# A hybrid decoder step on one core: last products deferred past the next first product, the input copied from the transposes' banks, a row ring of 13, prompt stores begun by ScalarE

## The chip, the core and the metric

The kernel runs on one core of a Trainium2 chip. TensorE (PE in the tables, its weight loads PEld), VectorE (DVE), ScalarE (ACT), GpSimd (POOL) and SyncE (SP, which here only begins DMAs) each run their own list of instructions in order and wait for one another by semaphores. Matrix products are collected in PSUM, eight banks of 128 x 512 floats; everything else lies in SBUF. The metric is the time of one execution on the device in microseconds (us).

## The reference, cut to what matters

```python
def hybrid_layer(x, pos0, n_lead, pool_buf, C, n, m, ...):
    hn = rmsnorm(x, norm_g)
    proj = jnp.einsum('btd,dn->btn', hn, w_in)
    a_pool, z_pool, q, k, v, o, z_m, i_pre, f_pre, g_pool, g_mlstm = split_projection(proj)
    y_pool = multiscale_pool(pool_buf, a_pool, pos0, w_pool, pool_scale) * jax.nn.silu(z_pool)
    ...
    (C_new, n_new, m_new), h = mlstm_scan(qh, kh, vh, ig, lf, state, n_lead)
    ...
    y_mlstm = jax.nn.sigmoid(o) * h.astype(x.dtype) * jax.nn.silu(z_m)
    u = (jax.nn.sigmoid(g_pool) * jnp.einsum('btp,pd->btd', y_pool, w_branch_pool)
         + jax.nn.sigmoid(g_mlstm) * jnp.einsum('btm,md->btd', y_mlstm, w_branch_mlstm))
    x_out = x + jnp.einsum('btd,de->bte', u, w_out)
```

There are 560 tokens (16 meta, 512 of a prompt, 8 samples of 4), a model width of 1024, 4 heads of 512, and an input projection of 1024 x 14344 in float32. The outputs are the tokens, and the new states: the prompt's memories C (one 512 x 512 for each head) and those of the 8 samples, which are read, updated and written back.

## The kernel before

**Arithmetic.** Each float32 operand is split into a high part (a ScalarE cast) and a low part (a VectorE subtraction), and each product is three products of parts (`mm3`, whose matmuls all bear L166). `hT` holds the normalised input, transposed, as such a pair.

**Units.** The input projection is cut into units of 256 output columns. 47 are a `quad`: seven block products in place of eight, each of 12 matmuls with 272 columns, on sums of quarters of the input (`S`, parts a to d, made once by `quarter_sums`) and sums of weight blocks. In the order of the code they are p1, p2, p6, p5, p7, p3, p4. Three banks carry them. The last one, p4 (weights `wb`, input `hT`), adds to bank A only after VectorE has read that bank for the total "22" (L253) and before ScalarE writes it out as "21" (L284). A total writes a tile that later goes to DRAM; where the tile's slot last held something that is being stored, VectorE waits for that store, and p4 for VectorE. The units of the v projection (L974, L977) are ordinary products.

**Stages.** `begin` normalises and transposes five tiles of tokens. The transposes stand in PSUM; `parts` in it casts `hT_hi` on ScalarE and subtracts `hT_lo` on VectorE from those banks (L80). `projections_begin` runs the first a unit, the gates (L573 and the single rows on four partitions, L577 to L641), the quarter sums and the v units of head 0, and the casts of z unit 0. `quarter_sums` first lets GpSimd add `hT_hi` and `hT_lo` to four tiles x (L539), then VectorE combine them (L542). `projections` walks over the other units; each is woven with the operands of the next, with the stores of the one before, and with the sample memories (`sample_C`, L1121 and L1130 on TensorE, L1135 on VectorE). `attention` runs the four heads, the pooling branch and the mLSTM branch follow, and the output product ends the kernel.

**Order.** TensorE's order inside the stages is that of the code (a manual schedule); `weave` interleaves lists of steps evenly. Instructions made through `Pinned` (`pA`, `pV`) keep the code's order too. The other engines are ordered by a scheduler, but each then runs its list strictly in order: an instruction that waits holds all behind it, and a DMA that SyncE cannot begin yet holds all later DMAs of SyncE.

**Rings.** Tiles are taken from rings of slots: "r" (12 slots of 128 x 560: q, k, v and c as they come or go, and y), "row" (9 slots of 128 x 544 in a head: `D2` with the denominators, `og` with the gated outputs, `sqn` with the squares). A new tile waits until the old one in its slot is done with. In a head, GpSimd sums the decay rows to `D2` (L1411 to L1416), these are split to dh and dl (L140), and TensorE sums them over partitions (L1399). The new prompt memory of a head is made in four row blocks: TensorE (L1358), a copy c32 by ScalarE (L1361), and a store begun by SyncE (L1362).

Of the kernel before, what the change touches and what calls it, by code (L numbers as in the profile page):

```python
# [23 lines left out]
H = 4  # L24
# [59 lines left out]
class Unit:  # L84
# [3 lines left out]
    def __init__(self, load=(), ahead=(), products=(), after=(), then=()):  # L88
        self.load, self.ahead, self.products = list(load), list(ahead), list(products)
        self.after, self.then = list(after), list(then)  # L90

# [8 lines left out]
class Trunk:  # L100
# [85 lines left out]
    def quad(self, src, lo, dst, scale=None, f21=None, after=(), then=()):  # L186
# [98 lines left out]
        return Unit([load], ahead, [p1, p2, p6, p5, p7, p3, p4], after, then)  # L285
# [77 lines left out]
    def begin(self):  # L363
# [29 lines left out]
        self.hT = [ip.tile([P, NK, NT], F32R, name=n) for n in ("hT_hi", "hT_lo")]  # L393
        self.hS = ip.tile([P, NK, 112], F32R, name="hS")
# [50 lines left out]
        def parts(*js):  # L445
            pieces = []
            for j in js:
                for q in range(2):
                    pv = pss[j, q].rearrange("p (k t) -> p k t", k=4)
                    for s, n, c0 in COLS[j]:  # L450
                        pieces.append((pv[:, :, s:s + n], *(t[:, 4 * q:4 * q + 4, c0:c0 + n] for t in self.hT)))
# [79 lines left out]
    def quarter_sums(self):  # L531
        nc = self.nc
        V, A, G = nc.vector, nc.scalar, nc.gpsimd
        steps, x = [], {}

        def load(k0, half, kh):
            t = x[half, kh] = self.gp.tile([P, 2, HN], F32, tag=f"x{half}{kh}", name=self.name("x"), bufs=1)
            hi, lo = (t[:, 4 * kh + k0:4 * kh + k0 + 2, HN * half:HN * half + HN].bitcast(F32) for t in self.hT)
# [12 lines left out]
        for k0 in (0, 2):  # L551
            steps += [lambda k0=k0, t=t: load(k0, *t) for t in (a, c, b, d)]
            steps += [lambda: sums(ALU.subtract, a, c, a), lambda: sums(ALU.subtract, c, b, c),
                      lambda: sums(ALU.subtract, b, a, b), lambda: sums(ALU.add, d, d, b)]
            for s, t in ("a", a), ("b", b), ("c", c), ("d", d):
                steps += [lambda k0=k0, s=s, t=t, l=l: part(k0, s, t, l) for l in (False, True)]
        return steps


    def gates(self):  # L560
# [22 lines left out]
        V.scalar_tensor_tensor(az, z, -1.0, z, ALU.mult, ALU.max)  # L583
# [39 lines left out]
        for i in (3, 2, 1, 0):  # L623
            own = TILE0[i] + P - TSTART[i]
            V.tensor_copy(sv[i][:, :own], nQ[:, TSTART[i]:TSTART[i] + own])

            V.tensor_scalar(sv[i][:, own:], sv[i + 1][:, :SEGW[i] - own],
                            b[:, TILE0[i] + P - 1:TILE0[i] + P], None, ALU.add)
            yield
        for i in range(5):  # L630
            c0 = TILE0[i]
            c1 = c0 + (P if i < 4 else 16)
            last = (SEGW[i] if i < 4 else 16) - 1
            V.tensor_scalar(wsr[:, c0:c1], a[:, c0:c1], sv[i][:, last:last + 1], None, ALU.add)
            yield
# [24 lines left out]
    def projections_begin(self):  # L660
# [7 lines left out]
        for f in v[0].ahead + a.products:  # L668
            f()
        for n, u in enumerate(v):  # L670
# [16 lines left out]
    def projections(self, rest):  # L687
# [46 lines left out]
        loaded, C, outs = 0, {}, []  # L734
# [5 lines left out]
        for t, u in enumerate(units):  # L740
# [20 lines left out]
        for f in before.after + old.then + before.then + outs:  # L761
            f()
# [186 lines left out]
    def unit_v(self, h):  # L949
# [8 lines left out]
        def part(kk, low):  # L958
# [3 lines left out]
            else:  # L962
                (G if h == 0 and kk % 2 else V).tensor_tensor(w[kk][2], w[kk][0], w[kk][1].bitcast(F32), ALU.subtract)
# [237 lines left out]
    def attention(self):  # L1201
# [15 lines left out]
        for h, u in enumerate(heads):  # L1217
# [21 lines left out]
    def head(self, h):  # L1239
# [15 lines left out]
        def row(name):  # L1255
            return self.hp.tile([P, NO], F32, tag="row", name=self.name(name), bufs=9)
# [96 lines left out]
        def prompt_C(d):  # L1353
# [8 lines left out]
            nc.sync.dma_start(O["C_prompt"][0, 0, h, d * P:(d + 1) * P], c32)  # L1362
# [134 lines left out]
    def y_in(self, yy, k, src):  # L1497
        nc = self.nc
        t = self.r("y32")[:, :NO]
        nc.sync.dma_start(t, src)  # L1500
# [12 lines left out]
    def pool_branch(self):  # L1513
# [12 lines left out]
        for k in range(8):  # L1526
            self.y_in(self.yp2, k, self.yp_d[:, k])
# [8 lines left out]
    def final(self, up):  # L1536
# [4 lines left out]
        for m in range(16):  # L1541
            y_in(ym[m // 8], m % 8, self.y_d[:, m])
# [96 lines left out]
```

## Time and profile before

| | |
|---|---|
| median of 3 runs | 1148.51 us (1145.27 to 1151.25) |
| the profiled execution | 1146.45 us, of which 1144.6 us are the span of its instructions |
| TensorE busy | 1066.5 us (93%) |
| VectorE busy | 843.0 us (74%) |
| ScalarE busy | 533.5 us (47%) |
| GpSimd busy | 195.2 us (17%) |
| DMA | 233.33 MB, mean 204 GB/s |

One execution was recorded. A line of the timeline gives an instruction's start and duration and, in brackets, how long its engine had stood idle before it and whose work released it. The view of waits adds these up; the view of windows gives each engine's busy time in a stretch and the clock granted to TensorE (1.00 is full speed, 0.50 half). The chain follows the work that ended last back to the start.

### The profile page before, as it was taken

How to read it: one execution, taken by the hardware profiler on the slowest of the kernel's cores; microseconds unless marked ns; L12 is line 12 of the kernel's file. 1: busy time of each engine (PE TensorE's matmuls, PEld its weight loads, DVE VectorE, ACT ScalarE, POOL GpSimd, SP SyncE). 2: the span in 40 equal slices, each digit the busy share in tenths (PEclk: the TensorE clock that was granted, in tenths of full speed). 3: DMA queues.
4: the chain of work that ended last, by engine and by line, in shares of the span. 5: the costliest groups of instructions: out<-in, count | busy, mean ns of one | idle time of the engine just before them, and what ended most of it. 6: DMA issues, size and time to landing. Idle time of an engine off the chain costs nothing.

```text
span 1144.6 us, 19677 instructions
## 1 busy us (share of the span) xinstructions
PE 1066.5 (93%) x7390; PEld 961.5 (84%) x7390; DVE 843.0 (74%) x1346; ACT 533.5 (47%) x1003; POOL 195.2 (17%) x323
## 2 busy tenths in 40 slices
PE   7948999998999999999998999986999789999997
PEld 5848999967999968999868989975978679999976
DVE  5696888796789697889696888863699888534353
ACT  4455555333554435554444554455677555222232
POOL 3720120001210000400001300022454534100000
PEclk9978999998999999999999999997999899999999
DMA  8424456779656778657588567887677699522232
GB/s 214 149 51 122 136 166 203 256 235 275 214 182 219 238 257 236 212 178 249 186 266 262 167 223 268 282 280 259 205 264 248 203 310 353 174 74 75 66 116 83
DMA packets 159663, 233.33 MB, mean 204 GB/s; under 512 B 17369, under 2 KB 82133, under 8 KB 159561
## 3 DMA queue, kind: packets, MB, share of 16 engines
q1 hardware_dynamic: 159569, 232.09, 63.2%
q8 instruction: 58, 0.95, 0.3%
q14 instruction: 36, 0.29, 0.1%
HBM read 160.65 MB, written 70.93 MB: 202 GB/s over the span
## 4 chain that ended last, share of the span: by engine, by line
PE 68%; DMA 11%; DVE 9%; issue 4%; ACT 3%; POOL 3%; SPq 1%; DVEq 0%; POOLq 0%; ACTq 0%
PE ps L166 55%; PE ps L974 4%; DMA v_d<-v 3%; PE ps L1121 2%; DMA wraw<-in_w_in_dram 2%; PE ps L1358 2%; PE ps L1130 1%; DMA kw<-k_d 1%; DMA out_dram<-C 1%; POOL x L539 1%; ACT qc L1156 1%; DMA k<-k_d 1%; PE ps L1401 1%; PE ps L977 1%; DMA ra<-in_w_in_dram 1%
## 5 line engine op out<-in xcount | busy, mean ns | idle before, releaser
L166 PE MATMUL ps<-hT_hi,w 128*128 128x272 f32 (+1 forms) x752 | 159.0, 297 | 0.0
L166 PEld LDWEIGHTS ps<-hT_hi,w 128*128 128x128 f32 x752 | 125.3, 193 | 4.2 <-issue 2.4
L166 PE MATMUL ps<-hT_lo,w 128*128 128x272 f32 (+1 forms) x376 | 110.2, 293 | 0.0
L1135 DVE SCALAR_TENSOR_TENSOR C<-C,sw,ps 128x512 f32<-128x512 f32 x128 | 89.4, 741 | 12.1 <-PE ps L1130 11.8
L166 PE MATMUL ps<-Sb_hi,wb 128*128 128x272 f32 (+1 forms) x376 | 80.9, 295 | 17.5 <-DVE wb L205 15.6
L166 PE MATMUL ps<-hT_hi,wb 128*128 128x272 f32 (+1 forms) x376 | 82.7, 299 | 11.4 <-DVE q L253 7.7
L1044 POOL COPY qm<-qw 128x16 f32<-128x16 f32 x32 | 7.1, 254 | 430.4 <-DVE qw L1041 430.4
L166 PE MATMUL ps<-Sa_hi,wa 128*128 128x272 f32 (+1 forms) x376 | 79.9, 292 | 0.0
L166 PE MATMUL ps<-Sc_hi,wa 128*128 128x272 f32 (+1 forms) x376 | 78.9, 290 | 0.0
L166 PEld LDWEIGHTS ps<-Sb_hi,wb 128*128 128x128 f32 x376 | 63.2, 192 | 18.7 <-issue 16.0
L166 PE MATMUL ps<-Sd_hi,w 128*128 128x272 f32 (+1 forms) x376 | 78.7, 289 | 0.0
L202 ACT CAST wa<-ra 128x1024 fp32r<-128x1024 f32 x47 | 49.4, 1050 | 62.0 <-DVE ra L215 55.4
L205 DVE TENSOR_TENSOR wb<-rb,wb 128x1024 fp32r<-128x1024 f32 x47 | 57.7, 1227 | 24.6 <-ACT wb L202 24.3
L166 PEld LDWEIGHTS ps<-hT_hi,wb 128*128 128x128 f32 x376 | 64.5, 195 | 13.1 <-DVE q L253 8.4
L166 PEld LDWEIGHTS ps<-hT_lo,w 128*128 128x128 f32 x376 | 72.6, 193 | 0.0
L202 ACT CAST w<-rb 128x1024 fp32r<-128x1024 f32 x47 | 49.3, 1050 | 29.3 <-PE ps L166 16.2
L166 PEld LDWEIGHTS ps<-Sa_hi,wa 128*128 128x128 f32 x376 | 63.0, 191 | 0.0
L166 PEld LDWEIGHTS ps<-Sc_hi,wa 128*128 128x128 f32 x376 | 62.2, 189 | 0.0
L166 PEld LDWEIGHTS ps<-Sd_hi,w 128*128 128x128 f32 x376 | 61.9, 188 | 0.0
L205 DVE TENSOR_TENSOR w<-rb,w 128x1024 fp32r<-128x1024 f32 x47 | 57.3, 1220 | 4.3 <-ACT w L202 4.3
L205 DVE TENSOR_TENSOR wa<-ra,wa 128x1024 fp32r<-128x1024 f32 x47 | 57.5, 1224 | 0.0
L166 PE MATMUL ps<-hT_lo,wb 128*128 128x272 f32 (+1 forms) x188 | 55.8, 297 | 0.0
(372 smaller groups left out, 3115.6 us busy)
## 6 DMA issues: line engine op xcount, KB each, us to landing
C<-in_state_C_dram SPq DMA_DIRECT2D x64, 512.0 KB
out_dram<-C SPq DMA_DIRECT2D x64, 512.0 KB
ra<-in_w_in_dram SPq DMA_DIRECT2D x47, 512.0 KB
rb<-in_w_in_dram SPq DMA_DIRECT2D x47, 512.0 KB
wraw<-in_w_in_dram SPq DMA_DIRECT2D x18, 512.0 KB
v<-v_d SPq DMA_DIRECT2D x32, 256.5 KB
wraw<-in_w_branch_mlstm_dram SPq DMA_DIRECT2D x16, 512.0 KB
k_d<-k SPq DMA_DIRECT2D x16, 280.0 KB
```

The lines of the kernel that those rows point to most:

```text
L166: self.nc.tensor.matmul(out, s, m, start=(first and j == 0), stop=(j == len(seq) - 1), skip_group_check=not check)
L202: A.copy(w[name][0], w[s])
L205: V.tensor_tensor(w[name][1], w[s], w[name][0].bitcast(F32), ALU.subtract)
L539: G.tensor_tensor(t, hi, lo, ALU.add)
L974: nc.tensor.matmul(pv[i], s, m[:, k2], start=(k == 0 and j == 0), stop=(k == 7 and j == 2))
L977: nc.tensor.matmul(pv[4][:112], self.hS[:, k], m[:, k2], start=(k == 0 and j == 0), stop=(k == 7 and j == 1))
L1121: nc.tensor.matmul(self.pqc[h][r:r + 8], self.qm[h % 2][:, d, b], Cs[bb // 2][:, bb % 2], start=(d == 0 and g == 0), stop=(d == 3 and g == 1),
L1130: nc.tensor.matmul(pu, self.kwst[h, d][r:r + 12, g], self.vst[h][r:r + 12, g], start=True, stop=True, tile_position=(r, 0))
L1135: V.scalar_tensor_tensor(C, C, self.bview(self.sw[h][:, 0])[:, 4 * g + bb, 3:4], pu, ALU.mult, ALU.add)
L1156: A.activation(t[r, :HD], pqc[r], AF.Copy, accum_out=t[r, HD:])
L1358: nc.tensor.matmul(pc, w[:, s, i], vr[i][:, m], start=(i == 0 and j == 0), stop=False)
L1401: nc.tensor.matmul(pb[:, o:o + mv.shape[-1] - m], s, mv[:, m:], start=(j == 0), stop=(j == last[True]))
```

## The change

Four things change.

- A `quad` gets the mark `tail`. `projections` emits the first product p1 of a unit, then the p4 kept back from the unit before, then the rest; sample products (`extra`) now stand ahead of the rest. The first unit there, z unit 0, has a transposition appended to its products, so that this is what is kept back, and its p4 stays in place.
- `begin` makes a tile `X` (128 x 8 x 560) with the whole input, by 12 ScalarE copies from the transposes' banks (8 of 128 x 512, 4 of 128 x 96), after the casts and the subtractions. `quarter_sums` drops its 8 GpSimd additions and works in place on `X`; the 4 low parts of b and d (L547) and 2 of the low parts of v weights (L963) go from GpSimd to VectorE. Four steps of the gates stand ahead of the v units.
- In the gates, |z| (L583), the four copies L625 and the five additions L634 go from VectorE to ScalarE.
- The row ring grows from 9 to 13. The 16 prompt stores L1362 are begun by ScalarE. In the last head, two loads of the pooling branch's input are begun ahead of the numerators, and the last of its `rows` steps is woven with them.

```diff
-        return Unit([load], ahead, [p1, p2, p6, p5, p7, p3, p4], after, then)
+        u = Unit([load], ahead, [p1, p2, p6, p5, p7, p3, p4], after, then)
+        u.tail = True
+        return u
...
+        self.X = gp.tile([P, NK, NT], F32, name="X")
...
-            for src, hi, lo in pieces:
+            for src, hi, lo, x in pieces:
                 pA.copy(hi, src)
-            for src, hi, lo in pieces:
+            for src, hi, lo, x in pieces:
                 pV.tensor_tensor(lo, src, hi.bitcast(F32), ALU.subtract)
+            for src, hi, lo, x in pieces:
+                pA.copy(x, src)
...
-            G.tensor_tensor(t, hi, lo, ALU.add)
+            x[half, kh] = self.X[:, 4 * kh + k0:4 * kh + k0 + 2, HN * half:HN * half + HN]
...
-                (G if s in "bd" else V).tensor_tensor(lo, x[t], hi.bitcast(F32), ALU.subtract)
+                V.tensor_tensor(lo, x[t], hi.bitcast(F32), ALU.subtract)
...
-        V.scalar_tensor_tensor(az, z, -1.0, z, ALU.mult, ALU.max)
+        nc.scalar.activation(az, z, AF.Abs)
...
-            V.tensor_copy(sv[i][:, :own], nQ[:, TSTART[i]:TSTART[i] + own])
+            nc.scalar.copy(sv[i][:, :own], nQ[:, TSTART[i]:TSTART[i] + own])
...
-            V.tensor_scalar(wsr[:, c0:c1], a[:, c0:c1], sv[i][:, last:last + 1], None, ALU.add)
+            nc.scalar.activation(wsr[:, c0:c1], a[:, c0:c1], AF.Identity, bias=sv[i][:, last:last + 1])
...
-        for f in v[0].ahead + a.products:
+        for f in v[0].ahead + a.products + other[:4]:
             f()
+        other = other[4:]
...
             products = u.products
+            for f in products[:1] + tail:
+                f()
+            products, tail = products[1:], []
+            if u.tail:
+                products, tail = products[:-1], products[-1:]
             if t not in values:
-                products, extra = products[:1] + extra + products[1:], []
+                products, extra = extra + products, []
...
-                (G if h == 0 and kk % 2 else V).tensor_tensor(w[kk][2], w[kk][0], w[kk][1].bitcast(F32), ALU.subtract)
+                V.tensor_tensor(w[kk][2], w[kk][0], w[kk][1].bitcast(F32), ALU.subtract)
...
-                weave(u.rows[-2:], u.sums, last)
-            weave(u.numerators[:-1] if h == H - 1 else u.numerators, m.keys + m.values)
+                weave(u.rows[-2:-1], u.sums, last)
+            if h == H - 1:
+                self.yraw = [self.y_load(self.yp_d[:, k]) for k in range(2)]
+                weave(u.numerators[:-1] + u.rows[-1:])
+            else:
+                weave(u.numerators, m.keys + m.values)
...
-            return self.hp.tile([P, NO], F32, tag="row", name=self.name(name), bufs=9)
+            return self.hp.tile([P, NO], F32, tag="row", name=self.name(name), bufs=13)
...
-            nc.sync.dma_start(O["C_prompt"][0, 0, h, d * P:(d + 1) * P], c32)
+            nc.scalar.dma_start(O["C_prompt"][0, 0, h, d * P:(d + 1) * P], c32)
```

In `begin`, ScalarE's row of casts before was this (`hT_hi` from the transposes; `wg` is the gates' weight, loaded by a DMA):

```order
L80 CAST hT_hi<-ps_262 128x4x128
L80 CAST hT_hi<-ps_267 128x4x128
L80 CAST hT_hi<-ps_297 128x4x24 x2
L80 CAST hT_hi<-ps_302 128x4x24 x2
L137 CAST wg<-wg_raw 128x8x64
L961 CAST whi_408<-wraw_120 128x1024
```

and is now, on the same engine at the same place:

```order
L80 CAST hT_hi<-ps_272 128x4x128
L80 COPY X<-ps_249 128x4x128
L138 CAST wg<-wg_raw 128x8x64
L80 COPY X<-ps_254 128x4x128
L80 COPY X<-ps_267 128x4x128
L80 COPY X<-ps_272 128x4x128
L80 CAST hT_hi<-ps_302 128x4x24 x2
L80 CAST hT_hi<-ps_307 128x4x24 x2
L80 COPY X<-ps_302 128x4x24 x2
L80 COPY X<-ps_307 128x4x24 x2
L553 CAST Sa_hi<-X 128x560 x2
```

The casts of the last token tile moved behind the cast of `wg` and three copies.

On TensorE, at the end of the first q unit of head 1 (p3 on `Sd`, p4 on `wb`, then p1 of the next unit; ps are banks), the rows before were:

```order
L166 MATMUL ps_2952<-Sd_lo,w_424_2777 128x272
L166 MATMUL ps_2952<-Sd_hi,w_424_2777 128x272
L166 MATMUL ps_2892<-hT_hi,wb_2838 128x272
L166 MATMUL ps_2892<-hT_lo,wb_2837 128x272
...
L166 MATMUL ps_2892<-hT_hi,wb_2837 128x272
L166 MATMUL ps_3035<-hT_hi,w_443_2858 128x272
L166 MATMUL ps_3035<-hT_lo,w_443_2858 128x272
```

and are now:

```order
L167 MATMUL ps_2952<-Sd_hi,w_417_2780 128x272
L167 MATMUL ps_3017<-hT_hi,w_435_2858 128x272
L167 MATMUL ps_3017<-hT_lo,w_435_2858 128x272
...
L167 MATMUL ps_3017<-hT_hi,w_435_2858 128x272
L167 MATMUL ps_2888<-hT_hi,wb_2835 128x272
L167 MATMUL ps_2888<-hT_lo,wb_2834 128x272
```

The 12 matmuls of p1 moved between p3 and p4.

On GpSimd, in the middle of `attention` (P are the decay matrices, D the row of denominators of head 2, klo low parts of keys), the rows before were:

```order
L140 TENSOR_TENSOR Pl_10326<-bc_9590,Ph_10325 128x144
L140 TENSOR_TENSOR Pl_10326<-bc_9590,Ph_10325 80x48
L140 TENSOR_TENSOR klo_10322<-k_1745_10319,khi_10321 128x560
L1411 TENSOR_TENSOR D_1764_10381<-bc_9590 128x400
L1412 COPY D_1764_10381<-bc_9590 128x112
L1413 COPY D_1764_10381<-qns 128x32
L140 TENSOR_TENSOR klo_10378<-k_1761_10375,khi_10377 128x560
L1416 TENSOR_TENSOR D_1764_10381<-D_1764_10381,bc_9590 128x272
```

and are now:

```order
L1425 TENSOR_TENSOR D_1756_10378<-bc_9587 128x400
L141 TENSOR_TENSOR Pl_10312<-bc_9587,Ph_10311 128x400
L1430 TENSOR_TENSOR D_1756_10378<-D_1756_10378,bc_9587 128x272
...
L1430 TENSOR_TENSOR D_1756_10378<-D_1756_10378,bc_9587 48x48
L141 TENSOR_TENSOR klo_10319<-k_1737_10316,khi_10318 128x560
L141 TENSOR_TENSOR klo_10375<-k_1753_10372,khi_10374 128x560
```

The whole sum of D moved ahead of the two keys, among the decay matrices.

## Rows read from the trace of the kernel before

**Rows 1.** The page: busy time, share of the span and instructions of TensorE.

```profile
PE 1066.5 (93%) x7390; PEld 961.5 (84%) x7390; DVE 843.0 (74%) x1346; ACT 533.5 (47%) x1003; POOL 195.2 (17%) x323
```

**Rows 2.** Waits of TensorE: line, releaser's line; total us, times, longest.

```profile
PE ps L166 <- DVE q L253: 7.7, 3, 3.5
...
PE ps L166 <- ACT p L238: 1.8, 3, 0.6
```

**Rows 3.** Windows: stretch, length, busy us by engine, clock, DMA share, GB/s.

```profile
97.00:272.00 175.00, 172.98 (x1230) 154.11 (x1230) 142.45 (x226) 84.08 (x146) 11.51 (x37) 0.98 0.62 196
778.00:800.00 22.00, 13.12 (x48) 9.75 (x47) 10.58 (x20) 11.58 (x28) 3.73 (x4) 0.69 0.88 287
...
945.00:1144.00 199.00, 191.45 (x1355) 180.16 (x1354) 98.49 (x148) 56.46 (x90) 23.11 (x29) 1.00 0.41 134
```

**Rows 4.** Timeline of TensorE: start, us, instruction, idle before and releaser.

```profile
82.70 0.57 PE L166 MATMUL ps<-Sb_hi,wb 128*128 128x272 f32 x1 [15.61 <-DVE wb L205]
94.67 0.39 PE L166 MATMUL ps<-hT_hi,wb 128*128 128x272 f32 x1 [3.00 <-DVE zx L253]
...
277.14 0.60 PE L166 MATMUL ps<-hT_hi,wb 128*128 128x272 f32 x1 [2.65 <-DVE q L253]
...
789.32 0.77 PE L166 MATMUL ps<-qh,klo 128*128 128x512 f32 x1 [5.44 <-ACT qh L137]
...
903.35 0.54 PE L1399 MATMUL ps<-dl,ones 128*128 128x240 f32 x1 [8.49 <-DVE dl L140]
935.33 0.82 PE L166 MATMUL ps<-yp,wlo 128*128 128x272 f32 x2 [4.71 <-ACT yp L137]
```

**Rows 5.** The chain that ended last: start, us, what (matmuls counted).

```profile
94.67 2.36 PE ps L166 x12
...
113.78 34.98 PE ps L166 x276
...
277.14 11.82 PE ps L166 x70
...
783.11 6.06 DMA out_dram<-c
```

**Rows 6.** Timeline of ScalarE, start of the kernel.

```profile
23.83 0.90 ACT L80 CAST hT_hi<-ps 128x96 fp32r<-128x96 f32 x4 [1.35 <-PE ps L80]
30.63 0.62 ACT L137 CAST wg<-wg_raw 128x512 fp32r<-128x512 f32 x1 [5.90 <-DMA wg_raw<-in_w_in_dram]
```

**Rows 7.** Timeline of VectorE, first 97 us.

```profile
32.31 1.40 DVE L963 TENSOR_TENSOR wlo<-wraw,whi 128x1024 fp32r<-128x1024 f32 x1 [5.50 <-ACT whi L961]
39.63 5.25 DVE L542 TENSOR_TENSOR x<-x,x 128x560 f32<-128x560 f32 x4 [5.92 <-POOL x L539]
44.79 0.73 DVE L547 TENSOR_TENSOR Sa_lo<-x,Sa_hi 128x560 fp32r<-128x560 f32 x1
...
57.76 1.93 DVE L583 SCALAR_TENSOR_TENSOR az<-zf 4x560 f32<-4x560 f32 x1
...
80.96 0.46 DVE L634 TENSOR_SCALAR ws<-ga,rw 4x128 f32<-4x128 f32 x2
81.35 1.21 DVE L205 TENSOR_TENSOR wb<-rb,wb 128x1024 fp32r<-128x1024 f32 x1
```

**Rows 8.** Timeline of SyncE: DMAs begun in the attention.

```profile
780.76 0.34 SPq L1362 DMA_DIRECT2D out_dram<-c  x1
...
931.13 0.35 SPq L1231 DMA_DIRECT2D out_dram<-np_out  x1
931.52 3.83 SPq L1500 DMA_DIRECT2D y<-yp_d  x8
```

**Rows 9.** Timeline of GpSimd in the attention.

```profile
893.68 1.45 POOL L1411 TENSOR_TENSOR D<-bc 128x400 f32<-128x400 f32 x1 [3.17 <-DVE og L1470]
...
896.48 1.84 POOL L140 TENSOR_TENSOR klo<-k,khi 128x560 fp32r<-128x560 f32 x1
```

**Rows 10.** The page: groups; line engine op, busy, mean ns, idle before.

```profile
L1135 DVE SCALAR_TENSOR_TENSOR C<-C,sw,ps 128x512 f32<-128x512 f32 x128 | 89.4, 741 | 12.1 <-PE ps L1130 11.8
```

More of the change, by code (lines that the diff above doesn't have):

```diff
@@ L90, in __init__ @@
         self.after, self.then = list(after), list(then)
+        self.tail = False
 def weave(*lists):
@@ L450, in parts @@
                     for s, n, c0 in COLS[j]:
-                        pieces.append((pv[:, :, s:s + n], *(t[:, 4 * q:4 * q + 4, c0:c0 + n] for t in self.hT)))
-            for src, hi, lo in pieces:
+                        pieces.append((pv[:, :, s:s + n], *(t[:, 4 * q:4 * q + 4, c0:c0 + n] for t in (*self.hT, self.X))))
+            for src, hi, lo, x in pieces:
                 pA.copy(hi, src)
-            for src, hi, lo in pieces:
+            for src, hi, lo, x in pieces:
                 pV.tensor_tensor(lo, src, hi.bitcast(F32), ALU.subtract)
+            for src, hi, lo, x in pieces:
+                pA.copy(x, src)
         def first(j):
@@ L534, in quarter_sums, with quarter @@
         steps, x = [], {}
-        def load(k0, half, kh):
-            t = x[half, kh] = self.gp.tile([P, 2, HN], F32, tag=f"x{half}{kh}", name=self.name("x"), bufs=1)
-            hi, lo = (t[:, 4 * kh + k0:4 * kh + k0 + 2, HN * half:HN * half + HN].bitcast(F32) for t in self.hT)
-            G.tensor_tensor(t, hi, lo, ALU.add)
+        def quarter(k0, half, kh):
+            x[half, kh] = self.X[:, 4 * kh + k0:4 * kh + k0 + 2, HN * half:HN * half + HN]
         def sums(op, out, p, q):
@@ L551, in quarter_sums @@
         for k0 in (0, 2):
-            steps += [lambda k0=k0, t=t: load(k0, *t) for t in (a, c, b, d)]
-            steps += [lambda: sums(ALU.subtract, a, c, a), lambda: sums(ALU.subtract, c, b, c),
+            steps += [lambda k0=k0: [quarter(k0, *t) for t in (a, c, b, d)], lambda: sums(ALU.subtract, a, c, a), lambda: sums(ALU.subtract, c, b, c),
                       lambda: sums(ALU.subtract, b, a, b), lambda: sums(ALU.add, d, d, b)]
@@ L733, in projections @@
         self.early = self.head(0)
-        loaded, C, outs = 0, {}, []
+        loaded, C, outs, tail = 0, {}, [], []
         before = Unit(after=rest[0].after + rest[1].after)
@@ L755, in projections @@
             products = u.products
+            for f in products[:1] + tail:
[3 more added lines that the diff above has]
+                products, tail = products[:-1], products[-1:]
             if t not in values:
-                products, extra = products[:1] + extra + products[1:], []
+                products, extra = extra + products, []
             weave(products, ahead, old.then + before.after, extra, done, self.gate_steps[t] if t < 2 else [])
             old, before = before, u
-        for f in before.after + old.then + before.then + outs:
+        for f in tail + before.after + old.then + before.then + outs:
             f()
@@ L1495, in both, with y_load, y_in @@
         return [pool.tile([P, 8, NO], F32R, tag="yy", name=f"{name}{j}", bufs=bufs) for j in range(2)]
-    def y_in(self, yy, k, src):
+    def y_load(self, src):
+        t = self.r("y32")[:, :NO]
+        self.nc.sync.dma_start(t, src)
+        return t
+    def y_in(self, yy, k, t):
         nc = self.nc
-        t = self.r("y32")[:, :NO]
-        nc.sync.dma_start(t, src)
         self.split(yy[0][:, k], yy[1][:, k], t, nc.scalar, nc.gpsimd if k % 2 else nc.vector)
```

4 lines of the change are left out of this document (2 added, 2 removed).

## The prediction, as it was recorded before the run

> **What bounds the kernel now.** I read the page first: TensorE is busy for 1066.5 of 1144.6 us [rows 1], so no edit that frees another engine pays unless it shortens one of TensorE's waits, or a stretch in which those waits have pulled its clock down. The 78 us without work are the whole stock. The waits of TensorE by releaser [rows 2] and its own timeline [rows 4] say where they lie; the windows [rows 3] say where they don't: from 97 to 272 us it is busy for 172.98 of 175, and from 945 us to the end at clock 1.00, so nothing that the change does elsewhere is worth anything there. The chain [rows 5] gives the price of a slow clock: 276 matmuls of the projections take 34.98 us, 0.127 each, while the 70 that follow the wait at 277.14 take 11.82, which is 11.82 - 70 x 0.127 = 2.9 too many. Four places are left: the end of the start (to 97 us), the three q waits, the first head of the attention, and the stretch from 893 to 945 us.
>
> **The start.** TensorE waits 15.61 us for the low part of `wb` and another 3.00 for zx before the last 12 matmuls, which end at 94.67 + 2.36 = 97.0 [rows 4, 5]. From the first of these waits' end that is 14.3 us for 60 matmuls; 60 x 0.127 are 7.6, the wait is 3.0, and the remaining 3.7 are slow clock.
>
> Against the change: ScalarE's cast of `wg` waits for a DMA and ends at 30.63 + 0.62 = 31.25 [rows 6]. The casts of the last token tile, which ended at 23.83 + 0.90 = 24.73, now stand behind it and three copies. A copy of 128 x 512 is not shown; the cast of this size took 0.62, so the casts end at about 31.25 + 3 x 0.62 + 0.9 = 34.0, 9.3 us later, and TensorE's products on those tokens wait for them. What hides this is the 15.61 us: 6.3 are left of them, some 3 if TensorE then runs at half clock for a while. The copies' sum, 8 x 0.62 + 0.9 = 5.9 us of ScalarE, lies in the same idle stretch.
>
> For it: VectorE's sums began at 39.63, after 5.92 us of waiting for GpSimd's additions [rows 7]. With the input in `X` they begin when the last copies are done, 34.0 + 0.9, so 4.7 us earlier. VectorE loses |z|, 1.93, and nine short gate rows at 0.46 / 2 = 0.23, 2.1 in all. It gains four low parts at 0.73 and two weight parts at 1.40, 5.7 in all. The eight sums took 5.25 for four beside GpSimd; the low part, of the same shape, took 0.73, so between nothing and 2 x (5.25 - 4 x 0.73) = 4.7 come back. The balance for `wb` is 4.7 + 1.9 + 2.1 - 5.7 = 3.0, up to 7.7 us earlier than 81.35. As TensorE's v products end later, and ScalarE must empty their banks between its casts, I take 2. Behind that, the 14.3 us shrink to 7.6 with neither wait nor slow clock, to 11.3 with the same clock; the tile that zx waits for is stored earlier by the same gate rows, and the idle time before is some 5 us and no longer 15.6, so I take 9.3. Gain 2 + 5 = **7**, from 0 (the later products eat both) to 7.7 + 6.7 = 14.
>
> **Deferred products.** Each quad's p4 now has the 12 matmuls of the next p1 ahead of it, 12 x 0.127 = 1.5 us of cover, and p6 has as much more behind p1. The three q waits sum to 7.7, the longest 3.5 and the one at 277.14 2.65, which leaves 1.55 for the third [rows 2, 4]: 3 x 1.5 = 4.5 are covered. The three waits on ScalarE's p, 1.8 in all, at most 0.6 each, vanish. Of the slow clock behind the q waits (2.9 at the one, none measured for the others in these rows) I give back 2. Sum **8**. It could be 4 if the next p1 is itself not ready, its weights being split by the same VectorE that waits; 11 with all the waits and the clock. Nothing is gained in the 172.98 busy us: the order alone changes there.
>
> **Stores begun by ScalarE.** SyncE reached the first memory's store and stood there until 780.76, ahead of loads of v, k and q [rows 8]; TensorE then waited 5.44 us for qh at 789.32 [rows 4], and the window 778 to 800 has it busy for 13.12 of 22.00 us at clock 0.69 [rows 3]. Without these stores in its row SyncE begins the loads some 2 to 3 us earlier. Gain taken **3**; at least 0, because a load of k also waits for the slot of a stored c, whose store took 6.06 us to land [rows 5]; at most 6, the wait and some clock. ScalarE pays 16 issues at SyncE's 0.34 each, 5.4 us; it is busy for 47% of the span [rows 1], so I put 1 on the path, and at most 5.4. Behind each store stand the casts of q, k and v; each waits for the copy that ScalarE has just made, and so for no other engine.
>
> The Trainium skill ("DMA: Bandwidth & Descriptors", section "Issuing engines are not separate DMA queues") says that DMAs begun by different engines run on the same 16 DMA engines, and that a second issuing engine saves only the time of the issue. By that rule the landing stays as it is, and this edit gives back only the blocked issue; no run here shows a store from ScalarE yet. It is rival 2 below.
>
> **The row ring.** In the middle of the attention TensorE stands 8.49 us for dl [rows 4]. GpSimd's D began at 893.68, 3.17 us after it was free, when VectorE had finished the og of an earlier head, whose slot it takes [rows 9]. With 13 slots that wait goes, and the order now sets the whole sum of D before the keys. What is late next is the second klo, 896.48 + 1.84 = 898.3, against 903.35 for dl: 5.0 us. Gain **5**; at least 3 (the 3.17 alone), at most 8.5.
>
> **The pooling branch.** TensorE waits 4.71 us for yp [rows 4]; the eight loads of y began at 931.52, after SyncE had waited with np_out until 931.13 [rows 8]. Two of them now go ahead. What is late next are the remaining loads, begun 3.83 / 8 = 0.5 us apart. Gain **3**, between 0 and 4.7 plus a little clock, 6.
>
> **Sum.** 7 + 8 + 3 - 1 + 5 + 3 = 25 us. The profiled execution took 1146.45, so 1121.5; that execution lay 2.06 below the median of the runs, of which I add a quarter: **1122**.
>
> **Rivals.**
>
> 1. *The start moves its wait and keeps it.* The 9.3 us that hT_hi is late, at half clock, use up the cover, and `wb` comes no earlier because two engines' work is now on VectorE. For it: the balance of 3.0 is small against its terms. Against: the cover is 15.61. Time: 1122 + 7 = 1129.
>
> 2. *Transfers set the pace of the attention.* The loads and stores share the same engines, the 778 to 800 window already has a DMA share of 0.88 [rows 3], and starting them earlier only makes them longer; then the 3, 5 and 3 of the attention go and the 1 for ScalarE stays. Against: D and yp wait for a slot and a blocked row, not for bytes. Time: 1122 + 11 = 1133. The page named above bears on this one.
>
> 3. *The deferral hides nothing.* VectorE is held by the same store when it should split the next unit's first weights, so p1 waits in place of p4. For it: all of it stands in one row on VectorE. Against: those parts are made during the unit before. Time: 1122 + 8 = 1130.
>
> 4. *Slower: banks.* A deferred p4 keeps bank A open while the next unit's A is already being filled, in every one of 46 units (47 quads, less z unit 0), beside the banks of the sample products, which VectorE empties at 741 ns each [rows 10]. If each unit waits for one such emptying, that is 46 x 0.741 = 34 us; the deferral's 8 go as well: 1122 + 34 + 8 = 1164. It decides from 17 / 46 = 0.37 us a unit, where it has used up the other gains. Against: before, with three banks to a unit, TensorE lost 2 us in the 175 from 97 to 272 us [rows 3], so banks are hardly short.
>
> 5. *More than forecast.* With the waits short the clock never falls: the upper ends of the start, the deferral and the row ring, 14 + 11 + 8.5 for 7 + 8 + 5, give 1122 - 13.5 = 1108.
>
> **How the numbers follow.** The forecast has 0.58 (its own range 1113 to 1131), rival 1 0.14, rival 2 0.08, rival 3 0.07, rival 4 0.05, rival 5 0.08. A time of two of rivals 1 to 3 together, 1137 to 1141, is not out of reach. The range, 1105 to 1140, leaves out rival 4 and the outer ends of 2 and 5. A measurement of this kernel tells 0.5% from no change, here 5.7 us: faster is below 1142.8, slower above 1154.3. From the cases: slower 0.05, all of it rival 4; same 0.07, the pile of rivals 1 to 3 and the low side of rival 4; faster 0.88.
>
> **What would show it.** In the profile after: a wait for `wb` of some 5 us and none for zx, with a new one of about 8 us before 35 us; q waits of about 1.2, 0.1 and 2.0 and none for ScalarE's p; the wait for dl near 3.5 and for yp near 2; the 945 us stretch as long as before (199 us for the same work). If TensorE's waits for VectorE's C or for its banks appear in the middle of the projections, rival 4 holds; if the attention's waits are the same with other DMAs as releasers, rival 2. I am wrong in the mechanism, whatever the time, if the gain lies in the last 200 us.

## The result, and the profile after

The changed kernel took 1138.07 us (median of 4 runs, 1132.86 to 1139.08) against 1149.77 us (1145.27 to 1151.25) in the same comparison: a ratio of 0.9896, 95% interval 0.9854 to 0.9938. It is faster by about 12 us, where 26 were forecast: the time lies in the stated range, and 14 us of the gain did not come.

The page of the profiled execution (1139.08 us) has this row, which answers to [rows 1]: TensorE's busy time did not fall, it rose by 4.1 us.

```profile
PE 1070.6 (94%) x7390; PEld 966.5 (85%) x7390; DVE 836.8 (74%) x1342; ACT 542.8 (48%) x1027; POOL 153.3 (13%) x309
```

The waits of TensorE after (line, releaser's line; total us, times, longest), against [rows 2]:

```profile
PE ps L167 <- ACT u L239: 8.6, 3, 5.1
PE ps L80 <- ACT hT_hi L80: 7.0, 2, 5.4
PE ps L1359 <- DVE kw L1341: 4.7, 1, 4.7
...
PE ps L167 <- DVE q L254: 4.0, 3, 2.8
PE ps L1413 <- DVE sl L141: 3.7, 1, 3.7
PE ps L1372 <- DVE bc L1385: 3.5, 1, 3.5
PE ps L167 <- DVE wlo L141: 3.5, 1, 3.5
...
PE ps L167 <- ACT p L239: 1.9, 2, 1.4
```

`q` fell from 7.7 to 4.0, `wb` from 15.6 to 0.6, and `dl` (8.5) is gone from the list. In their place stand waits that were not in it before (u, sl, and bc at L1372; wlo has the place of yp) or were small (hT_hi 0.2, kw 1.6). The waits for p did not vanish, as was forecast: 1.9 us stand against 1.8, of which 1.42 are new, at the first p6. Lines after L88 of the changed kernel have moved; L1359 is the old L1345, L1372 the old L1358, L1413 the old L1399, L1315 the old L1301. Heads are counted from 0: head 1 is the second head.

The windows after (stretch, length, busy us of TensorE, its loads, VectorE, ScalarE, GpSimd, then clock, DMA share, GB/s), laid on about the same work as [rows 3]:

```profile
87.00:262.00 175.00, 173.55 (x1251) 154.79 (x1250) 145.09 (x231) 84.78 (x148) 12.20 (x37) 1.00 0.65 203
768.00:790.00 22.00, 14.03 (x60) 10.63 (x59) 11.30 (x23) 13.05 (x34) 4.69 (x7) 0.77 0.95 299
937.00:1136.00 199.00, 192.09 (x1360) 180.70 (x1358) 99.83 (x148) 56.91 (x90) 23.29 (x29) 1.00 0.41 133
```

The middle of the projections and the last 199 us are as busy as before (173.55 and 192.09 us); the first head of the attention has 14.03 busy us of 22 where it had 13.12.

The timeline of TensorE after, its waits at the places of [rows 4] and the new ones (start, us, instruction, idle before and releaser):

```profile
33.49 0.62 PE L80 MATMUL ps<-hT_hi,whi 128*128 128x304 f32 x1 [5.37 <-ACT hT_hi L80]
...
77.97 0.39 PE L167 MATMUL ps<-Sb_hi,wb 128*128 128x272 f32 x1 [1.42 <-ACT p L239]
90.51 0.39 PE L167 MATMUL ps<-Sb_hi,wb 128*128 128x272 f32 x1 [0.62 <-DVE wb L206]
...
283.81 0.60 PE L167 MATMUL ps<-Sc_hi,wa 128*128 128x280 f32 x1 [5.10 <-ACT u L239]
...
782.89 1.09 PE L1359 MATMUL ps<-ident,kw 128*128 128x128 f32 x4 [4.68 <-DVE kw L1341]
...
832.14 5.49 PE L1372 MATMUL ps<-vr,kwr 128*128 128x512 f32 x12 [3.53 <-DVE bc L1385]
...
906.74 0.54 PE L1413 MATMUL ps<-sl,ones 128*128 128x240 f32 x1 [3.67 <-DVE sl L141]
...
928.07 0.60 PE L167 MATMUL ps<-yp,wlo 128*128 128x272 f32 x1 [3.50 <-DVE wlo L141]
```

From such rows, the same work can be laid side by side. The table gives the start of the same matmul in both profiled executions; the last column is their difference, the gain gathered so far.

| place | before | after | gain |
|---|---|---|---|
| p6 of z unit 0 | 82.70 | 77.97 | 4.7 |
| p6 of the next unit | 103.08 | 90.51 | 12.6 |
| head 1, p6 of the first k unit | 295.88 | 275.47 | 20.4 |
| head 1, p6 of the second k unit | 306.83 | 293.76 | 13.1 |
| head 2, p6 of the first k unit | 460.72 | 445.64 | 15.1 |
| head 2, p6 of the second k unit | 471.67 | 461.14 | 10.5 |
| last unit's p6 | 752.85 | 742.37 | 10.5 |
| attention, memory of head 1 | 841.64 | 832.14 | 9.5 |
| attention, numerators of head 1 | 853.50 | 846.90 | 6.6 |
| attention, dl of head 2 | 903.35 | 892.24 | 11.1 |
| attention, sl of head 2 | 914.33 | 906.74 | 7.6 |
| pooling branch, first matmul | 935.33 | 928.07 | 7.3 |
| end of the span | 1144.6 | 1137.3 | 7.3 |

The start gave more than forecast. The deferral gave its 8 us by 275 us and lost them again within one unit. The attention won 4.5 us at dl and lost 3.9 before it and 3.8 behind it.

Each column is one execution. The two differ by 7.3 us where the medians differ by 11.7: the one before, 1146.45 us, lay 3.3 below its median here, the one after 1.0 above. The start too differs between executions: in the eight profiled ones that have these edits of the start, the second unit's p6 begins at 89.64 to 92.48 us, a gain of 10.6 to 13.4.

The losses at 283.81 and 832.14 are more than their waits, because TensorE runs slowly behind each. At 832.14 above, the 12 matmuls of the memory take 5.49 us; the same 12 took 2.93 at 841.64 before. Behind 283.81 the granted clock was 0.54 for 5 us, near half speed. The row of before, and the window of after:

```profile
841.64 2.93 PE L1358 MATMUL ps<-vr,kwr 128*128 128x512 f32 x12
```

```profile
284.00:289.00 5.00, 5.00 (x23) 5.00 (x24) 3.31 (x6) 1.10 (x2) 0.00 (x0) 0.54 0.81 256
```

The chain after, at head 1 (start, us, what):

```profile
276.50 6.32 DMA ra<-in_w_in_dram
...
283.81 16.30 PE ps L167 x108
```

108 matmuls in 16.30 us are 2.6 us more than at 0.127 us each.

### The profile page after: what moved, and what is told of

Its sections match the earlier page's. It is cut to its first block, busy times and chain, and to the rows that moved or that the text cites. A ratio compares the mean times of both kernels' runs of the same rounds, so it can differ in the third digit from the quotient of the medians.

```text
span 1137.3 us, 19654 instructions
## 1 busy us (share of the span) xinstructions
PE 1070.6 (94%) x7390; PEld 966.5 (85%) x7390; DVE 836.8 (74%) x1342; ACT 542.8 (48%) x1027; POOL 153.3 (13%) x309
## 4 chain that ended last, share of the span: by engine, by line
PE 68%; DMA 14%; DVE 8%; ACT 5%; issue 3%; SPq 2%; POOL 0%; DVEq 0%; ACTq 0%; POOLq 0%
PE ps L167 55%; PE ps L984 4%; DMA out_dram<-C 2%; PE ps L1131 2%; DMA wraw<-in_w_in_dram 2%; DMA ra<-in_w_in_dram 2%; DMA v_d<-v 1%; DMA kw<-k_d 1%; PE ps L1140 1%; PE ps L1415 1%; DMA rb<-in_w_in_dram 1%; PE ps L80 1%; DMA v<-v_d 1%; PE ps L1372 1%; DMA bc<-rows_d 1%
## 5 line engine op out<-in xcount | busy, mean ns | idle before, releaser
L167 PE MATMUL ps<-hT_hi,wb 128*128 128x272 f32 (+1 forms) x376 | 79.9, 291 | 4.0 <-DVE q L254 4.0
L1372 PE MATMUL ps<-vr,kwr 128*128 128x512 f32 x192 | 52.6, 431 | 6.9 <-DVE bc L1385 3.5
```

What stands on the lines that cost most here:

```text
L167: self.nc.tensor.matmul(out, s, m, start=(first and j == 0), stop=(j == len(seq) - 1), skip_group_check=not check)
L1372: nc.tensor.matmul(pc, w[:, s, i], vr[i][:, m], start=(i == 0 and j == 0), stop=False)
```

## The experiments

Each is compared with the kernel before by a ratio of times that were measured together; the kernel before had medians of 1149.77 to 1153.1 us in them. Theory S: behind the waits for q the weights' loads are late, because of SyncE's row. The rows on which it rests are, after the change, SyncE's (start, us for so many DMAs, line):

```profile
266.02 5.40 SPq L1019 DMA_DIRECT2D vst<-vs_d  x6
...
276.50 0.43 SPq L196 DMA_DIRECT2D ra<-in_w_in_dram  x1
```

ScalarE's, at the same place:

```profile
275.78 0.40 ACT L285 ACTIVATE q<-ps 128x272 f32<-128x272 f32 x1
282.84 0.62 ACT L210 CAST w<-ra 128x512 fp32r<-128x512 f32 x1 [6.65 <-DMA ra<-in_w_in_dram]
283.36 0.40 ACT L239 ACTIVATE u<-ps 128x280 f32<-128x280 f32 x1
```

The weight block `ra` of the second k unit is begun at 276.50, behind six vst loads that take SyncE 5.40 us to begin, and lands 6.32 us later. ScalarE's cast of it (L210) stands ahead of the copy u of the unit at work, so TensorE waits for u: 5.10 us at 283.81. No run moved that cast behind u, so what the order on ScalarE alone would give back is not shown. Between the two `ra` loads SyncE is occupied almost without a gap.

### e1: the deferral alone

```diff
+            for f in products[:1] + tail:
+                f()
...
+            if u.tail:
+                products, tail = products[:-1], products[-1:]
```

> The kernel before with the deferred last products alone. Theory S (the weights' loads set the pace where a head's q and k units follow its v units: they stand in SyncE's row behind some 14 us of other DMAs, so TensorE waits there whatever its own order is): the three waits for q shrink to under 1.2, new waits for ScalarE's u of 2 to 5 us come one or two units later, and the total is the same within 2 us, 1148 to 1152. Theory D (the deferral gains its 8 us by itself and only loses them when the start is shortened as well): 1141 to 1144, with no wait for u over 1 us.

1153.99 us, ratio 1.0017 (0.9998 to 1.0036). Theory D falls: the deferral alone gains nothing. Of theory S the time and the waits for u came, the fall of the waits for q did not: they sum to 6.4 us and not to less than three times 1.2, and the longest, at head 3, is 4.0. Its waits (the start's wait for `wb` is that of the kernel before):

```profile
PE ps L167 <- DVE wb L206: 15.6, 1, 15.6
PE ps L167 <- ACT u L239: 9.0, 3, 4.8
...
PE ps L167 <- DVE q L254: 6.4, 3, 4.0
```

### e2: the edits of the start alone

```diff
-            G.tensor_tensor(t, hi, lo, ALU.add)
+            x[half, kh] = self.X[:, 4 * kh + k0:4 * kh + k0 + 2, HN * half:HN * half + HN]
```

(with the copies to `X`, the gates' moves and the low parts on VectorE)

> The kernel before with the edits of the start alone (input copied from the banks, gates and low parts moved). The place of p6 in the second unit stood 12.6 us earlier in the changed kernel. If the start's gain reaches the end unhindered: 1137 to 1138. Theory S: the units' waits at the head changes are the same as before, so nothing of it is lost there: 1137 to 1139. Theory D: the earlier start runs into the loads and loses 5 or more: 1142 to 1145.

Ratio 0.9877 (0.9847 to 0.9906), 1136.86 us: the whole change is no faster than this part. The start's gain reaches the end, less 2.1 us that are lost on the way through the projections (10.6 at the second p6, 8.5 at the last), where the waits for q sum to 8.5 us and those for p to 3.2, against 7.7 and 1.8 before.

### e3: the edits of the attention alone

```diff
-                weave(u.rows[-2:], u.sums, last)
+                weave(u.rows[-2:-1], u.sums, last)
...
-            return self.hp.tile([P, NO], F32, tag="row", name=self.name(name), bufs=9)
+            return self.hp.tile([P, NO], F32, tag="row", name=self.name(name), bufs=13)
...
-            nc.sync.dma_start(O["C_prompt"][0, 0, h, d * P:(d + 1) * P], c32)
+            nc.scalar.dma_start(O["C_prompt"][0, 0, h, d * P:(d + 1) * P], c32)
```

> The kernel before with the edits of the attention alone (row ring 13, stores begun by ScalarE, two loads ahead, last head woven otherwise). In the changed kernel the attention and the entry into the pooling branch took 3.2 us more than before. Theory C (GpSimd's sums, let go by the ring, run beside VectorE's instructions and stretch them, and the chain over VectorE is longer for it): 1151 to 1154, that is 2 to 4 us over the kernel before. Theory P (the edits gain their 10 us, and lose them only because the start and the deferral bring TensorE to the attention too early for its loads): 1139 to 1143.

Ratio 0.9997 (0.9977 to 1.0017), 1151.67 us: neither theory's number; the edits neither gain 10 nor lose 3. In place of dl (8.5) stand waits that the kernel before did not have (sl, wlo) or had smaller (kw, 1.6):

```profile
PE ps L1403 <- DVE sl L140: 5.4, 1, 5.4
...
PE ps L1349 <- DVE kw L1331: 3.8, 1, 3.8
...
PE ps L166 <- DVE wlo L140: 3.5, 1, 3.5
```

The three parts multiply to 0.9877 x 1.0017 x 0.9997 = 0.9891, the whole has 0.9896: within the intervals the three parts simply add up.

### e4: the vst loads begun by GpSimd

```diff
-                nc.sync.dma_start(vst[r:r + 12, b // 4].bitcast(F32), vt["d"][:, 4 * b:4 * b + 4])
+                nc.gpsimd.dma_start(vst[r:r + 12, b // 4].bitcast(F32), vt["d"][:, 4 * b:4 * b + 4])
```

> The changed kernel with the 32 loads of vst (stacked sample values) begun by GpSimd instead of SyncE. Their issue took 0.7 to 0.9 us each in SyncE's row, six in 5.40 us just ahead of the weights' load that came too late. Theory S: the weights' loads of the k units are begun some 5 us earlier, the waits for u (5.10 and 2.90 us) fall under 1 us, and the time falls by 6 to 9 us against the changed kernel, to 1129 to 1132. Rival A (the wait for u is a matter of ScalarE's row, where a cast that waits for a later weight stands ahead of u, or of the transfers' bandwidth): waits unchanged, 1137 to 1140.

1127.49 us, ratio 0.9791 (0.9765 to 0.9817): some 11 us below the changed kernel, more than the 6 to 9 of theory S. The same place, first SyncE's row and the chain, then GpSimd's row, then TensorE's waits:

```profile
271.63 0.39 SPq L196 DMA_DIRECT2D ra<-in_w_in_dram  x1
```

```profile
271.63 6.64 DMA ra<-in_w_in_dram
```

```profile
265.05 3.37 POOL L1019 DMA_DIRECT2D vst<-vs_d  x6 [108.04 <-PE ps L167]
```

```profile
261.20 0.39 PE L167 MATMUL ps<-hT_hi,wb 128*128 128x272 f32 x1 [1.16 <-DVE q L254]
279.27 0.40 PE L167 MATMUL ps<-Sc_hi,wa 128*128 128x280 f32 x1 [1.12 <-ACT u L239]
```

The load is begun 4.9 us earlier. It takes no less time to land (6.64 us, 6.32 in the changed kernel), so it is the beginning that came earlier, not a faster transfer. The wait for u is 1.12 instead of 5.10 us (under 1 was expected), the one of 2.90 us at head 2 is gone, and the gain over the kernel before stands at 21.1 us when the projections end (10.5 in the changed kernel). GpSimd had been idle for 108 us there.

### f1: the same, without the deferral

```diff
-            for f in products[:1] + tail:
-                f()
...
             if t not in values:
-                products, extra = extra + products, []
+                products, extra = products[:1] + extra + products[1:], []
```

> The kernel with the vst loads begun by GpSimd (1127.5 us), with the deferral undone. Theory S (the deferral is worth its 8 us once the weights' loads are in time): the waits for q return to 1.6 to 4 us each and those for p to 0.6, and the time rises to 1134 to 1137. Rival (the vst loads alone made the gain, and the deferral is worth nothing in any setting): 1126 to 1129.

1134.92 us, ratio 0.9858 (0.9826 to 0.9891): 7.4 us more than e4, and the intervals do not overlap. Its waits, and the one for q in e4:

```profile
PE ps L167 <- DVE q L254: 7.7, 3, 3.2
...
PE ps L167 <- ACT p L239: 3.2, 4, 1.4
```

```profile
PE ps L167 <- DVE q L254: 6.0, 3, 4.2
```

In the profiled executions 2.4 us of the difference stand already at the second unit's p6 (92.04 and 89.64), where the start varies; from there to the last unit's p6 e4 gains 6.4 us on f1. Shorter waits are less than half of these: 7.7 against 6.0 us for q, 3.2 against 1.4 for p, with 1.1 for u in e4 alone, and the longest wait for q, at head 3, is not covered at all (3.2 here, 4.2 in e4). Much of the rest is the clock behind the shortened waits. At head 1 TensorE waits 2.83 us for q in f1 and 1.16 in e4; the 7 us from there have 42 matmuls at clock 0.76 in f1 and 54 at 1.00 in e4:

```profile
265.00:272.00 7.00, 6.80 (x42) 6.81 (x43) 5.83 (x10) 3.17 (x5) 5.02 (x10) 0.76 0.97 307
```

```profile
261.00:268.00 7.00, 6.80 (x54) 6.80 (x55) 5.84 (x11) 3.90 (x7) 2.88 (x6) 1.00 0.99 280
```

So the deferral is worth about the 8 us that were forecast, where the loads are in time.

### g1: the vst loads on the kernel before

The edit is that of e4, on the kernel before.

> The kernel before with the 32 vst loads begun by GpSimd and nothing else. Theory S (before, TensorE's own wait for q came first and gave SyncE's row the time that it needed; the row becomes the bound only when that wait is covered): within 3 us of the kernel before, 1148 to 1152, with the three waits for q still there. Rival (the row was a bound by itself, and the 10 us of the vst change have nothing to do with the deferral): 1140 to 1143.

1150.09 us, ratio 0.9978 (0.9962 to 0.9995): 2.5 us less. Alone, neither the deferral (e1) nor these loads (g1) is worth much. As theory S reads it, TensorE's own wait for q had given SyncE's row the time it needed.

### f2: centring the last rows of v on ScalarE

```diff
-                V.tensor_scalar(v[:80], v[:80], mean[:80], None, ALU.add)
+                A.activation(v[:80], v[:80], AF.Identity, bias=mean[:80])
```

Theory C, for the attention, rests on this VectorE instruction, in the second head before and after:

```profile
838.91 1.34 DVE L1301 TENSOR_SCALAR v<-v,vs 80x512 f32<-80x512 f32 x1
```

```profile
827.64 3.44 DVE L1315 TENSOR_SCALAR v<-v,vs 80x512 f32<-80x512 f32 x1
```

and on what GpSimd did in the same 3.4 us after:

```profile
827.54 1.04 POOL L1425 TENSOR_TENSOR D<-bc 128x400 f32<-128x400 f32 x1
828.55 2.24 POOL L141 TENSOR_TENSOR Pl<-bc,Ph 128x512 fp32r<-128x512 f32 x2
```

> The kernel with the vst loads begun by GpSimd, with the four additions that centre the last rows of v (80 x 512, L1315) on ScalarE instead of VectorE. Theory C (this VectorE instruction stands still while GpSimd works: 3.44 and 2.31 us where 0.4 is its shortest; it holds the next banks' evictions and the loads that stand behind its result in SyncE's row): the wait before the second head's memory goes, and the time falls by 2 to 5 us, to 1122 to 1125. Rival (VectorE is slowed by GpSimd all the same, in its other instructions, or the chain moves to ScalarE): 1126 to 1130.

1124.7 us, ratio 0.9772 (0.9741 to 0.9803). The medians differ by 2.8 us, as theory C has it; the intervals of e4 and f2 overlap, so the size is not settled. In the changed kernel TensorE waited 3.53 us for bc before the second head's memory. In e4, which differs in the vst loads alone, that is 1.20 us already, and L1315 takes 2.31 us; in f2 the addition takes ScalarE 0.72 us, and there is no wait for bc there, but one of 2.18 us for kwst. The memory begins at 820.81 instead of 821.40; counted from the last unit's p6, at 732.40 and 731.79, that is 1.2 us earlier. More is not seen in this stretch.

### f3: the row ring back at 9

Against e4:

```diff
-            return self.hp.tile([P, NO], F32, tag="row", name=self.name(name), bufs=13)
+            return self.hp.tile([P, NO], F32, tag="row", name=self.name(name), bufs=9)
```

> The kernel with the vst loads begun by GpSimd, with the row ring back at 9. As predicted (the ring is worth 5 us): 1131 to 1134, with the wait of 8 us for dl back. Theory C (what the ring gives back at dl it loses where GpSimd then runs beside VectorE): 1125 to 1129, with the wait for dl back and those for sl and for the second head's memory smaller.

1128.73 us, ratio 0.9811 (0.9777 to 0.9846) against 0.9791: the wait for dl is back (8.2 us in two), that for sl (5.6) is gone, and the total is the same within the intervals. The forecast's 5 us for the ring are not seen: the medians differ by 1.2 us, and e3, which has the ring among its edits, gained nothing.

### f4: the prompt stores back on SyncE

Against e4:

```diff
-            nc.scalar.dma_start(O["C_prompt"][0, 0, h, d * P:(d + 1) * P], c32)
+            nc.sync.dma_start(O["C_prompt"][0, 0, h, d * P:(d + 1) * P], c32)
```

> The kernel with the vst loads begun by GpSimd, with the 16 prompt stores begun by SyncE again. As predicted (3 us less 1): 1129 to 1130, with the wait for qh at the first head back at 4 to 5 us and the new wait for kw (5.08 us) smaller. Rival (the loads that SyncE begins earlier only wait for the slots of c, whose stores land when they land, so the wait moves from qh to kw): 1126 to 1129.

1124.23 us, ratio 0.9770 (0.9741 to 0.9799): no loss, and rather a gain than a loss. At the first head the wait only changes its name, as the rival had it: with ScalarE's stores TensorE waits 1.14 and 1.93 us for qh and 5.08 for kw, with SyncE's 1.43 and 4.25 for qh and 2.00 for kw. A store can also stand in ScalarE's row. In e4, the fourth copy of c, its store, and the cast behind it:

```profile
766.58 0.58 ACT L1375 COPY c<-ps 128x512 f32<-128x512 f32 x1 [1.15 <-DMA out_dram<-c]
...
771.11 0.34 ACTq L1376 DMA_DIRECT2D out_dram<-c  x1
771.76 0.65 ACT L138 CAST qh<-q 128x544 fp32r<-128x544 f32 x1 [4.04 <-DMA q<-q_d]
```

The copy ended at 767.16, the store began at 771.11 and the cast of q behind it at 771.76. In the order of the instructions this store waits for a DMA's semaphore beside that of the copy. By the row the cast waited last for its own load of q, so that this store cost ScalarE's row anything is not shown.

### h1: the attention's edits without the moved stores

The edit is that of f4, on e3.

> The kernel before with the edits of the attention alone, but with the prompt stores left on SyncE. The attention edits together gave no change (ratio 0.9997), and with the vst loads on GpSimd the stores on ScalarE cost 3.3 us. If the stores cost the same here: 1147 to 1150, that is 2 to 4 us below the kernel before in the same call, with the second and fourth store no longer waiting on ScalarE. If ring and last head give nothing either, and the 3.3 us were a matter of the other edits: 1151 to 1154.

1149.86 us, ratio 0.9977 (0.9959 to 0.9995) against 0.9997 for e3. It points the same way as f4, the stores on ScalarE costing some 2 us; the two intervals overlap.

### g2 and g3: the parts together, and an earlier last token tile

g2 has the edits of e4, f2 and f4 together.

> The changed kernel with the vst loads begun by GpSimd, the four additions L1315 on ScalarE and the prompt stores back on SyncE. If the three add up: 1127.5 - 2.8 - 3.3 = 1121 to 1122. If the last two take away the same wait (VectorE's row before the second head's memory): 1124 to 1125.

1126.04 us, ratio 0.9771 (0.9744 to 0.9798): f2 and f4 do not add. With both, the wait for sl in the third head is 7.0 us (2.6 and 3.0 in f2 and f4).

```diff
+            copies.extend((x, src) for src, hi, lo, x in pieces)
+            if js[0] in (0, 1, 4):
+                for x, src in copies:
+                    pA.copy(x, src)
```

> The same as g2_combo, with the casts and subtractions of the last token tile ahead of the cast of the gates' weight, the copies X of the third and fourth tile behind it. If the wait of 5.4 to 9.3 us for hT_hi at 33 us is on the path (TensorE is busy without a gap from there to p6): 4 to 8 us less than g2_combo, 1114 to 1118. If, as predicted, the idle time before wb hides it: the same as g2_combo within 2 us, with a wait for wb in its place.

1127.62 us, ratio 0.9777 (0.9748 to 0.9806): the same as g2. g3 makes the copies to `X` later. In g2 TensorE waited for the casts,

```profile
34.40 0.62 PE L80 MATMUL ps<-hT_hi,whi 128*128 128x304 f32 x1 [5.96 <-ACT hT_hi L80]
```

in g3 it waits 1.82 us there, for a copy to `X`, but `wb` is then late:

```profile
75.44 0.36 PE L167 MATMUL ps<-Sb_hi,wb 128*128 128x272 f32 x1 [3.25 <-DVE wb L206]
```

p6 begins 3.4 us earlier and the projections end 3.6 us earlier; the end of the runs does not show it. All versions with the vst loads on GpSimd and the stores on SyncE, or L1315 on ScalarE, lie at 0.977 to 0.978, 10 to 14 us below the changed kernel. They have the lowest medians here, though their intervals overlap with that of e4.

## Why the prediction was right and wrong

**The start: right, and larger.** 7 were forecast, 12.6 stand in the table at the second p6, and 1.2% in e2. The places were right: hT_hi waits (5.37 us where some 8 were expected), the wait for zx is gone, and the 60 matmuls of z unit 0 take 77.97 to 86.2, 8.2 us, where 9.3 were taken for the old 14.3. Two terms were too small. `wb` was forecast from the low end of 3.0 to 7.7; it came 5.7 us earlier (75.69 against 81.35). VectorE was ready still earlier: beside an idle GpSimd four sums took 2.73 us, against 5.25 in [rows 7] and the 4 x 0.73 = 2.92 of that term's upper bound. It then stood 4.02 us for ScalarE's cast of `wb`, which came behind ScalarE's copies of v and the additions that had moved there:

```profile
34.67 2.73 DVE L546 TENSOR_TENSOR X<-X 128x560 f32<-128x560 f32 x4 [0.45 <-ACT X L80]
...
75.69 1.23 DVE L206 TENSOR_TENSOR wb<-rb,wb 128x1024 fp32r<-128x1024 f32 x1 [4.02 <-ACT wb L203]
```

And the unit behind, which had run at a low clock before (0.55 from 97 to 103 us), gave 1.7 more. That the idle time hides the late hT_hi was wrong: there was no idle time left before p6, which waited 1.42 us for its own unit's p, in ScalarE's row. Rival 1 had that half right, and the other wrong: `wb` did come earlier. Taking most of the hT_hi wait away (g3) brought a wait for `wb` instead, of 3.25 us.

**The deferral: the term that failed.** The size, 8 us, was right (f1 against e4: 7.4; the table: 12.6 to 20.4), with one of the three waits not covered: 3.46 us for q at head 3 before, 2.82 in the changed kernel and 4.20 in e4; why it stays was not followed. The step that failed is the one that counts a covered wait as gained ("3 x 1.5 = 4.5 are covered"). The prediction asked only whether the next unit's p1, split by VectorE, would be ready, and set the price of that at 4 us of 8. What was late next was the weights' load of the unit behind, held in SyncE's row, through a cast on ScalarE that stands ahead of u. It took all 8. The trace of before had the rows. SyncE's, at head 1:

```profile
275.21 0.40 SPq L195 DMA_DIRECT2D ra<-in_w_in_dram  x1
...
279.75 5.45 SPq L1009 DMA_DIRECT2D vst<-vs_d  x6
...
289.94 0.38 SPq L195 DMA_DIRECT2D ra<-in_w_in_dram  x1
```

Six vst loads are begun in 5.45 us, and 14.73 us lie between the begins of two `ra` loads, where TensorE's p6 of two units stand 10.95 us apart (295.88 and 306.83 in the table). SyncE's row is the longer of the two there. The prediction read the queue of SyncE for the attention only, where the change touched it, and not where the change made TensorE faster. Rival 3 has the loss of these 8 us, but by another mechanism, and its time, 1130, lies 8 us below the measured one.

**The ring: the wait went, the time did not.** dl fell from 8.49 to 0.46 us or less, more than the 5 forecast for it. In f3 nothing clear of the noise hangs on it. The step that failed is again what is late next: klo was named, and it was sl, a low part that VectorE makes in the same head, 3.67 us at 906.74; and GpSimd's sums now fall on VectorE's work, L1315 taking 3.44 us in place of 1.34. That the second is a cause of the loss at 832.14 (bc, 3.53 us) is not settled: f2 takes it away, and the memory then begins 1.2 us earlier.

**The stores: the gain is not there.** +3 and -1 were forecast; f4 and h1 point some 2 to 3 us the other way, but in both pairs the intervals overlap, and g2 against f2 shows no difference (0.9771 and 0.9772). "Each waits for the copy that ScalarE has just made, and so for no other engine" was wrong: the fourth store of e4 stood 3.95 us behind its copy, for a DMA, though its cost is not shown. At the first head the lower bound named in the prediction (a load waits for a slot of c, whose store must land) is what happened: in the changed kernel the load of kw was begun at 777.14, after SyncE had stood for such a store 5.6 us, and TensorE waited 4.68 us for kw at 782.89.

**The pooling branch.** 4.71 us for yp became 3.50 us for a weight's low part (wlo), which VectorE makes: what was late next was not the remaining loads. 3 were forecast; in the table the gain does not grow there, it goes from 7.6 to 7.3.

**Rival 2 and the page behind it.** The Trainium skill ("DMA: Bandwidth & Descriptors", "Issuing engines are not separate DMA queues") says that another issuing engine saves the issue alone. The traces agree as far as they go: the second store of c in head 0, begun by ScalarE, landed after 5.50 us in e4 (6.06 before, begun by SyncE), the `ra` load after 6.64 us in e4 (6.32 in the changed kernel). It does not follow that little is saved: with 32 loads out of SyncE's row the kernel was some 11 us shorter. As a mechanism, rival 2 was not isolated: no run took bytes away from the attention, and the window of its first head has a DMA share of 0.95 after, 0.88 before.

**Rival 4** did not happen: no wait for VectorE's C or for a bank is in the list, and the middle window is as full as before.

**The chances.** 0.14 + 0.08 + 0.07 were given to single failures of a term and only the range's end to two at once. The deferral and the attention failed wholly, for the same reason, and the start was larger: 1121.5 + 8 + 10 - 5.5 = 1134 by the parts, against 1138. The remaining 4 us are no more than executions of one kernel differ by (1132.86 to 1139.08). That two of rivals 1 to 3 together, 1137 to 1141, meet the measured time is luck: the start, which rival 1 makes smaller, gave more than forecast, and rival 3 has another cause.

## What to carry to other kernels

A wait that is covered can show the next one: before counting it as gained, follow each row that feeds the same place (here the DMA queue that begins the weights) and compare its length per unit of work with that of the engine which becomes faster. A full queue need not show as a wait while its consumer waits for something else: the kernel before had no wait for u at head 1, where SyncE's row was already the longer one. Moving a DMA gives back its issue time in the row that is full, and in the row to which it goes it can stand in the way, so look for an engine that is idle there; here GpSimd had been idle for 108 us.

## What the runs showed of the hardware

VectorE's addition of one scalar per partition to 80 x 512 floats took between 0.38 and 3.44 us in one run; the longest lasted from 827.64 to 831.08, while GpSimd ran tensor operations from 827.54 to 830.79. Four sums of 128 x 560 took VectorE 2.73 us beside an idle GpSimd, and 5.25 in the kernel before, beside a working one and on other tiles. Which of the two made the difference was not separated. A vst load took SyncE 0.68 us (median of 32) to begin, and GpSimd 0.56 us.
